# Two-layer decoder trunk on one core: eight wide expert places instead of twelve, ten expert groups instead of eleven, and the next layer's first weights prepared inside the expert stage

## The chip, the cores and the metric

The kernel runs on one core of a Trainium2 chip. The metric is the device time of one execution in microseconds (us). A trace of one execution shows for every engine what ran when: TensorE (PE, with its weight loads as PEld), VectorE (DVE), ScalarE (ACT), GpSimd (POOL), and SyncE (SP), whose queue issues nearly all transfers from device memory.

## The reference

Two layers over 256 tokens of width 1024, all in float32. Each layer mixes tokens (a combined projection, differential attention, sparse attention over 64 chosen keys, two gated branches, an output projection), normalises, and then runs a mixture of experts:

```
def hierarchical_moe(x, w_rg, b_rg, w_re, b_re, w_g, w_u, w_d):
    ...
    within = jnp.sum(jax.nn.one_hot(e_idx, EXPERTS_PER_GROUP, dtype=jnp.float32) * e_val[..., None], axis=1)
    comb = jax.nn.one_hot(g_idx[:, 0], N_GROUPS, dtype=jnp.float32)[:, :, None] * (g_val * within)[:, None, :]
    y = jnp.zeros_like(xt)
    for g in range(N_GROUPS):
        hg = jax.nn.silu(jnp.einsum('nd,edf->nef', xt, w_g[g])) * jnp.einsum('nd,edf->nef', xt, w_u[g])
        y = y + jnp.einsum('nef,efd->nd', hg * comb[:, g, :, None].astype(hg.dtype), w_d[g])
    return y.reshape(B, S, D)
...
        ple = jax.nn.sigmoid(x @ w_ple_gate[i]) * (p[i] @ w_ple[i])
        x = layer_norm(ALPHA * x + ffn + ple, ln2_g[i], ln2_b[i])
```

Every token goes to two of 32 experts (4 groups of 8; first one group, then two experts in it). On the reference's inputs the routing, worked out on the host from the reference alone, gives these tokens per expert. First layer: experts 0 to 3 have 45, 20, 35, 15; the four fullest of the others 45, 39, 28, 25; the next 23. Second layer: 13, 11, 12, 6; then 39, 39, 33, 32; the next 28.

## The kernel before

**Weights and places.** All weights lie in `ws` as blocks of 128 x 1024 float32, 512 KB each. The on-chip memory is cut into 47 places of that size (`Arena`, `Held`). A load takes the place that has been free longest (`load=True`); anything else takes one freed recently (`young=4` from the newest). SP issues the loads in one order, and each waits until the last reader of its place is done; what stands behind it in the queue waits too.

**The expert stage.** Experts are ranked: the first `NFIX` experts keep ranks 0 to 5 by number, so that their weights can be loaded before the routing is known, and the others follow by how many tokens they have. Ranks below `NBIG` have 64 columns, the others 32. A group fills 128 columns: two experts of 64 (12 loads) or four of 32 (24 loads). With 12 wide ranks that makes six groups of two and five of four, taken in the order `order`. Whatever does not fit in the columns is done by a loop over all experts, `leftover`, which is skipped when nothing is left over.

Each turn `gi` of the group loop runs on PE: `front(gi + 1)` (64 products of gate and up weights, which need 4 loads for each expert), `back(gi)` (32 products of the down weights, 2 loads for each expert), the gathering of the tokens for group `gi + 2`, and the combination of the group's result into the sums `ya` in PSUM. At some turns (`e1`, `early`, `lastat`) it also runs `Embed` units: a quarter of the per-layer embedding, two loads each and one more for two of them. `Embed(0)` is loaded early, and `nemb` says how many more are loaded before the routing is known.

**Before the routing is known** SP issues the loads of the fixed ranks and the early embeddings. Then it waits for `ids`, the ranks in a row, which `value_load` reads (L1034).

**End of a layer.** In the turn before the last, `wide` (L379) loads the two vectors of the second normalisation (queue line L382); POOL spreads them over the partitions. In the last turn the first four loads of the next layer's first projection are issued (`ahead`). Behind the last products the sums are normalised (`Norm`, L402 to L414), turned (L95), and the next layer's first projection begins. Each of its eight weight blocks is split into a rounded part and a rest (`parts`, `split`, L208 and L209): ACT makes the first, and here POOL the second.

Of the kernel before, what the change touches and what calls it, by code (L numbers as in the profile page):

```python
# [21 lines left out]
D = 1024  # L22
S = 256
DEPTH = 2
P = 128
KT = D // P
# [15 lines left out]
FAR = 1000.0  # L42


NFIX = 6
NBIG = 12


SEC = ["iq", "sq", "sk", "sv", "dq", "dk", "dv", "ga0", "ga1", "gb0", "gb1"]
# [30 lines left out]

@with_exitstack
def tile_hybrid_trunk(ctx: ExitStack, tc: tile.TileContext, x_in, xT_in, pT_in, pos_in, ws, wik, wrt, lnv,
                      brt, lamv, sublnv, out, places=47, t2b=4, young=4, gsb=1, hTb=1, silb=2, nring=5, early=(4, 5, 6), nahead=4, apart=8, npre=36, wA=1, wB=1, wC=1, wD=1, wE=3, inorder=2, e0=2, e1=2,  nearly_=0, peng_=1, ifat=3, im=0, df=0, dh=15, nol=0, diag=1, rpool='0000', lastemb=1, lastat=6, pre_if=(4,5), npair=6, fh=False, fg=0, order=(0,1,2,6,3,7,4,8,5,9,10), engs=None, nemb=1, nwarm=9, nfine=2, nah=4, o1=False, o2=False, o3=True, o4=True, order2=True, pa=2, pb=7, f1=True):
    nc = tc.nc
    V, A, G = nc.vector, nc.scalar, nc.gpsimd

    class Tensor:

        last = None
# [9 lines left out]
    def behind(*instructions):  # L99

        c = ExitStack()
        for i in instructions:
            if i is not None:
                c.enter_context(tc.issue_after(i.ins))
        return c

    def in_turn():

        return tc.issue_after(PE.last.ins)
# [14 lines left out]
    def bank():  # L124
        return ps.tile([P, 512], F32, tag="mm", bufs=4, name=nm("mm"))

    def wt(shape, dt, tag, bufs):
        return wk.tile(shape, dt, tag=tag, bufs=bufs, name=nm(tag))
# [3 lines left out]
    class Held:  # L132
# [11 lines left out]
        def free(self):  # L144
            arena.give(self.b)
# [16 lines left out]
    def load(l, i, shape):  # L162
        r = Held(shape, load=True)
        nc.sync.dma_start(r.t, ws[l, i])
        return r
# [41 lines left out]
    def split(hi, lo, src, eng=V):  # L207
        copied[0] = A.activation(hi, src, AF.Copy)  # L208
        copied[1] = eng.tensor_tensor(lo, src, hi, op=OP.subtract)  # L209
# [12 lines left out]
    ahead, ready = [], []  # L222
    nearly, peng = nearly_, peng_
# [30 lines left out]
    def constants():  # L254
# [14 lines left out]
        G.iota(kbon, pattern=[[-1, NE]], base=NE - 1, channel_multiplier=0, allow_small_or_imprecise_dtypes=True)  # L269
        V.tensor_scalar(kbon[:, :NFIX], kbon[:, :NFIX], 1.0e6, None, op0=OP.add)  # L270
        G.iota(kid[:, 0:1], pattern=[[0, 1]], base=0, channel_multiplier=1, allow_small_or_imprecise_dtypes=True)
        V.tensor_scalar(kid[:, 1:2], kid[:, 0:1], float(NFIX), 1.0e6, op0=OP.is_lt, op1=OP.mult)
        V.tensor_tensor(kid[:, 1:2], kid[:, 1:2], kid[:, 0:1], op=OP.subtract)
# [52 lines left out]
    def parts(w, ring=None, eng=V, old=False):  # L326

        if ring:
            ring.append(ring.pop(0))
        r = Held([2, 512], F32R, load=old, place=ring[-1] if ring else None)  # L330
        split(r.v[:, 0, :], r.v[:, 1, :], w, eng)
        return r
# [45 lines left out]

    def wide(i, l):  # L379

        r = Held([D])
        nc.sync.dma_start(r.v[0:1], lnv[l, i:i + 1])  # L382
        G.partition_broadcast(r.v, r.v[0:1])  # L383
        return r
# [68 lines left out]
    for l in range(DEPTH):  # L453
# [3 lines left out]
        ahead, ready = [], []  # L457
# [252 lines left out]
                free(*gates[:2])  # L710
        free(yaT, ybT)
        lng, lnb = wide(0, l), wide(1, l)
        wr36 = Held([KT, 36])
        nc.sync.dma_start(wr36.v, wrt[l])
        o = [None, None]
        for h in range(2):
# [161 lines left out]
        groups = [[(r, 2, 64)] for r in range(0, 2 * npair, 2)]  # L878
        small = NBIG
        for r in range(2 * npair, NBIG):  # L880
            n = min(2, NE - small)
# [69 lines left out]
        places = bank()  # L951
# [5 lines left out]
        with in_turn():  # L957
            places_of(places, mkf[:, :, :NFIX], slice(0, NFIX))
        gs = marks_of(0)
        with tc.issue_after(marked[0].ins):  # L960
# [24 lines left out]
            V.tensor_scalar(perm, iom[:NE, :NE], FAR, kcol[:, 2:3], op0=OP.add, op1=OP.is_equal)  # L985
            V.tensor_copy(cw[:, :, :NFIX], cbf[:, :, :NFIX])
        with in_turn():
# [8 lines left out]
        cmi = ids[:, NE:]  # L996
        V.tensor_scalar(ids[:, :NFIX], iom[0:1, :NFIX], FAR, None, op0=OP.add)
        V.tensor_copy(ids[:, NFIX:NE], b[0:1, 2 * NE + NFIX:3 * NE])
        over = cut(NE, rows=1)
        for c, n in (slice(0, NBIG), 64.0), (slice(NBIG, NE), 32.0):  # L1000
            V.tensor_scalar(over[:, c], b[0:1, 3 * NE + c.start:3 * NE + c.stop], n, None, op0=OP.subtract)
# [61 lines left out]
        def halves_of(yp):  # L1063
            y = t2([P, 512], F32R), t2([P, 512], F32R)
            split(*y, yp)
            return y
# [48 lines left out]
                        fetch(r, j)  # L1115
        for q in range(1, 1 + nemb):
            emb[q] = Embed(q)

        def strips(gi):


            for i, (_, sl) in enumerate(experts(gi)):
                for c in range(sl.start, sl.stop, 32):
                    yield i, slice(c, c + 32)
# [16 lines left out]
        def back(gi, hT):  # L1141

            ysplit.clear()
            ysplits.clear()
            wr = weights_of(gi, range(4, 6))
            if gi == last and l < DEPTH - 1:
                ahead.extend(load(l + 1, i, [2, 512]) for i in range(len(ahead), KT // 2))
                ready.extend(parts(r.v[:, k, :], eng=G) for r in ahead[:nearly] for k in range(2))
            ys = []
            for h in range(2):  # L1150
                yp = bank()
                for f in range(2):
                    for i, sl in strips(gi):
                        PE.matmul(yp[sl, :], hT[:, f, sl], wr[f][i].v[:, h, :], start=f == 0, stop=f == 1)
                ys.append(halves_of(yp))
                ysplits.append(copied[0])
                ysplit.append(copied[1])
            free(*wr[0], *wr[1])
            return ys

        last = len(groups) - 1
        ysplit, ysplits, powers = [], [], []
# [20 lines left out]
        def leftover(most):  # L1183
# [3 lines left out]
            with tc.If(most > 0, preferred_fallthrough_block=False):  # L1187
                onward(slice(0, NBIG), -64)
                onward(slice(NBIG, NE), -32)
                with tc.For_i(0, 2, 1):  # L1190
                    with tc.For_i(0, NE, 1) as r:
                        rest(r)
                    onward(slice(0, NE), -P)
                onward(slice(0, NBIG), 64 + 2 * P)
                onward(slice(NBIG, NE), 32 + 2 * P)
# [8 lines left out]
        for gi in range(len(groups)):  # L1204
            if gi == ifat:
                most = nc.values_load(cmi[0:1, 0:1], min_val=0, max_val=S)
            here = lambda: tc.manual_schedule(engines={mybir.EngineType.PE})
            with here():
                after = front(gi + 1, *slots) if gi < last else None
            if gi == ifat:  # L1210
                leftover(most)
            with here():
                ys = back(gi, hT)
                if gi + 2 <= last:
                    marks, slots = marks_of(gi + 2), Gathered(gi + 2 >= fg)
                    for k4 in range(2):
                        gather(marks, slots.half[k4], k4)
                units = embeds(gi)
                for e, t, some in units[:1]:
                    e.products(t, some)  # L1220
                if gi < last:
                    hT = turned(after[0], wt([P, 2 * P], F32, "hT", hTb))
                    for h in range(2):
                        for t in range(TT):
                            combine(ys[h], sT, h, t)
                    sT = after[1]
                for e, t, _ in units[:1]:
                    e.gate(t)
                for e, t, some in units[1:]:
                    e.products(t, some)  # L1230
                    e.gate(t)
                if gi + 2 <= last:
                    slots = slots, *ways_of(gi + 2, marks)
                for e, t, _ in units:
                    e.add(t)
            if gi == last - 1:
                lng, lnb = wide(2, l), wide(3, l)
                xn = [Held([D]) for _ in range(TT)]
                if l < DEPTH - 1:
                    xT = Split(KT)  # L1240
# [24 lines left out]
            ends[t:] = [norm.apply(t, o2)]  # L1265
            powers.append(power)
        lasts = copied[:]
        if l < DEPTH - 1:
            for k in range(KT):
                with behind(ysplits[min(k, 1)], powers[0] if k >= pa else None, powers[1] if k >= pb else None):  # L1270
                    ready.append(parts(ahead[k // 2].v[:, k % 2, :], eng=G, old=True))
            free(*ahead)

        free(lng, lnb, *x)
        x = xn

# [66 lines left out]
```

## Time and profile before

| | |
|---|---|
| three runs: median, lowest, highest | 939.35, 938.26, 940.98 us |
| the profiled execution | 940.85 us, of which 939.2 us span |
| PE busy | 906.3 us (96% of the span) |
| DVE, ACT, POOL busy | 425.7, 347.9, 33.8 us |
| bytes moved | 280.86 MB, 299 GB/s in the mean |

The expert stages lie from about 225 to 460 us and from about 687 to 926 us. PE counts as busy while a product runs or waits in its pipeline, so that 96% says little of what it waits for. The profile's row of GB/s shows where transfers run at their highest rate (about 416 GB/s) and where they do not.

### The profile page before, as it was taken

The page shows a single profiled execution, that of the slowest core. Times are in us where ns is not written, and L with a number is a line of the kernel's source. Part 1 is how long each engine was busy: PE and PEld are TensorE (multiplying, and loading weights), DVE is VectorE, ACT ScalarE, POOL GpSimd, SP SyncE. Part 2 cuts the span into 40 slices and gives each one's busy share as a digit, 9 for nine tenths or more (in the row PEclk, how much of TensorE's full clock was granted, in tenths as well). Part 3 has the DMA queues.
Part 4 walks back from the last instruction along what each step waited for, and adds up shares of the span by engine and source line. Part 5 has one row for each costly group of instructions (what it writes and reads, how often), then busy time and mean ns, then how long its engine had stood idle before and what let it go on. Part 6 is the DMA issues. An engine that isn't in the chain of part 4 may idle for free. (4 is left out here: it accounts for less than half of the span.)

```text
span 939.2 us, 15942 instructions
## 1 busy us (share of the span) xinstructions
PE 906.3 (96%) x5761; PEld 604.4 (64%) x5761; DVE 425.7 (45%) x1068; ACT 347.9 (37%) x704; POOL 33.8 (4%) x37
## 2 busy tenths in 40 slices
PE   8999999999999999999899999999989999999994
PEld 5877777876556466554388777788855465666441
DVE  6797466775221111122468954668731212112124
ACT  6567676532211111111346666775221111111110
POOL 0000000000000000000410000001000000000010
PEclk9999999999999999999999999999999999999998
DMA  8995343777899999996999233357778999999943
GB/s 280 414 405 202 115 144 127 248 235 286 304 380 385 412 418 416 416 415 273 387 418 364 90 125 123 113 186 252 251 278 322 360 417 414 418 419 416 418 177 139
DMA packets 79013, 280.86 MB, mean 299 GB/s; under 512 B 9160, under 2 KB 9928, under 8 KB 78928
## 3 DMA queue, kind: packets, MB, share of 16 engines
q1 hardware_dynamic: 78784, 279.78, 77.9%
q8 instruction: 47, 0.77, 0.3%
q14 instruction: 38, 0.31, 0.1%
q10 hardware_dynamic: 144, 0.00, 0.0%
HBM read 278.70 MB, written 1.05 MB: 298 GB/s over the span
## 5 line engine op out<-in xcount | busy, mean ns | idle before, releaser
L92 PE MATMUL acc<-a,a 128*128 128x512 f32 x1440 | 352.3, 398 | 2.7 <-ACT a L208 2.0
L92 PEld LDWEIGHTS acc<-a,a 128*128 128x128 f32 x1440 | 265.7, 188 | 65.5 <-ACT a L208 3.3
L92 PE MATMUL mm<-a,a 128*32 128x512 f32 (+5 forms) x1776 | 237.6, 526 | 0.0
L208 ACT ACTIVATE a<-a 128x512 fp32r<-128x512 f32 (+1 forms) x247 | 150.7, 631 | 100.2 <-PE acc L92 69.2
L209 DVE TENSOR_TENSOR a<-a,a 128x512 fp32r<-128x512 f32 (+1 forms) x239 | 160.1, 690 | 51.2 <-ACT a L208 50.5
L92 PEld LDWEIGHTS mm<-a,a 128*32 128x32 f32 (+3 forms) x1776 | 110.7, 130 | 99.2 <-issue 86.8
L92 PE MATMUL mm<-a,hT 128*32 128x512 f32 x704 | 96.4, 603 | 8.8 <-DMA a<-ws 4.9
L92 PEld LDWEIGHTS mm<-gs,a 128*128 128x128 f32 x704 | 80.4, 192 | 17.2 <-PE mm L92 11.7
L92 PE MATMUL mm<-gs,a 128*128 128x128 f32 x704 | 84.7, 278 | 0.0
L1050 ACT ACTIVATE sil<-mm 128x256 f32<-128x256 f32 x22 | 8.4, 383 | 171.5 <-PE mm L92 156.2
L92 PEld LDWEIGHTS mm<-a,hT 128*32 128x32 f32 x704 | 25.3, 111 | 71.4 <-issue 55.9
L1051 DVE SCALAR_TENSOR_TENSOR sil<-sil,wsl,mm 128x256 f32<-128x256 f32 x22 | 10.6, 481 | 133.6 <-ACT sil L1050 133.4
L209 DVE TENSOR_TENSOR t<-mm,t 128x512 fp32r<-128x512 f32 x44 | 30.4, 692 | 68.6 <-ACT t L208 68.6
L208 ACT ACTIVATE t<-mm 128x512 fp32r<-128x512 f32 x44 | 26.3, 597 | 78.6 <-PE mm L92 78.6
L919 DVE CAST sT<-mm 128x256 fp32r<-128x256 f32 x22 | 9.3, 425 | 97.4 <-PE mm L92 97.4
L92 PE MATMUL acc<-t,sT 128*128 128x512 f32 x176 | 48.4, 410 | 0.0
L906 ACT ACTIVATE a<-mm 128x512 f32<-128x512 f32 x40 | 23.9, 597 | 50.1 <-PE mm L92 47.6
L92 PEld LDWEIGHTS acc<-t,sT 128*128 128x128 f32 x176 | 31.1, 189 | 9.0 <-issue 2.5
L763 DVE TENSOR_TENSOR sil<-sil,mm 128x256 f32<-128x256 f32 x16 | 6.7, 416 | 54.4 <-ACT sil L762 54.4
L548 ACT ACTIVATE t<-mm,mx 128x128 f32<-128x128 f32 (+1 forms) x64 | 26.0, 421 | 10.7 <-DVE mx L545 10.7
L762 ACT ACTIVATE sil<-mm 128x256 f32<-128x256 f32 x16 | 6.1, 383 | 63.7 <-PE mm L92 63.7
L383 POOL PARTITION_BROADCAST a<-a x8 | 10.6, 1356 | 511.0 <-DMA a<-lnv 279.6
(197 smaller groups left out, 644.6 us busy)
## 6 DMA issues: line engine op xcount, KB each, us to landing
a<-ws SPq DMA_DIRECT2D x523, 512.0 KB, 9.4
a<-x_in SPq DMA_DIRECT2D x2, 512.0 KB
out<-a SPq DMA_DIRECT2D x4, 256.0 KB, 2.7
a<-xT_in SPq DMA_DIRECT2D x3, 256.0 KB
a<-wik SPq DMA_DIRECT2D x2, 288.0 KB, 8.2
a<-ws SPq DMA_DIRECT2D x2, 256.0 KB, 4.3
pT<-pT_in SPq DMA_DIRECT2D x2, 256.0 KB
a<-wrt SPq DMA_DIRECT2D x2, 144.0 KB, 2.7
```

Source lines behind the costliest of these rows:

```text
L92: self.last = nc.tensor.matmul(*a, **k)
L208: copied[0] = A.activation(hi, src, AF.Copy)
L209: copied[1] = eng.tensor_tensor(lo, src, hi, op=OP.subtract)
L383: G.partition_broadcast(r.v, r.v[0:1])
L548: A.activation(e[:, i * nk:(i + 1) * nk], b[:, i * nk:(i + 1) * nk], AF.Exp, bias=mx[:, i:i + 1], accum_out=sums[i])
L762: A.activation(g, b[:, :256], AF.Sigmoid)
L763: V.tensor_tensor(g, g, b[:, 256:], op=OP.mult)
L906: A.activation(xg, b.rearrange("p (k s) -> p k s", k=4), AF.Copy)
L919: V.tensor_copy(sT, b[:, :2 * P].rearrange("p (t q) -> p t q", t=TT))
L1050: A.activation(sil, gu[:, :FE], AF.Sigmoid)
L1051: V.scalar_tensor_tensor(sil, sil, wsl, gu[:, :FE], op0=OP.mult, op1=OP.mult)
```

## The change

Four ranks instead of six are fixed and eight instead of twelve have 64 columns. That makes four groups of two experts and six of four: ten groups. The three later embeddings are loaded before the routing is known and run one turn earlier, and so are the next layer's four first loads. The split of these is done in turns 6 and 7 by ACT and DVE, and no longer after the last group by ACT and POOL. The vectors of both normalisations and the routing weights (`wide`, `wr36`) take the longest free place, as loads do.

```
-NFIX = 6
-NBIG = 12
+NFIX = 4
+NBIG = 8
...
-  early=(4, 5, 6), lastat=6, pre_if=(4,5), npair=6, order=(0,1,2,6,3,7,4,8,5,9,10), nemb=1
+  early=(3, 4, 5), lastat=5, pre_if=(6,7), npair=4, order=(0,1,2,4,3,5,6,7,8,9), nemb=3
...
     def wide(i, l):
-        r = Held([D])
+        r = Held([D], load=True)
...
-        wr36 = Held([KT, 36])
+        wr36 = Held([KT, 36], load=True)
...
         for q in range(1, 1 + nemb):
             emb[q] = Embed(q)
+        if l < DEPTH - 1:
+            ahead.extend(load(l + 1, i, [2, 512]) for i in range(KT // 2))
...
             wr = weights_of(gi, range(4, 6))
-            if gi == last and l < DEPTH - 1:
-                ahead.extend(load(l + 1, i, [2, 512]) for i in range(len(ahead), KT // 2))
-                ready.extend(parts(r.v[:, k, :], eng=G) for r in ahead[:nearly] for k in range(2))
...
                 for e, t, _ in units:
                     e.add(t)
+            if l < DEPTH - 1 and gi in pre_if:
+                for r in ahead[:2] if gi == pre_if[0] else ahead[2:]:
+                    ready.extend(parts(r.v[:, k, :]) for k in range(2))
+                    r.free()
             if gi == last - 1:
...
         lasts = copied[:]
-        if l < DEPTH - 1:
-            for k in range(KT):
-                with behind(ysplits[min(k, 1)], powers[0] if k >= pa else None, powers[1] if k >= pb else None):
-                    ready.append(parts(ahead[k // 2].v[:, k % 2, :], eng=G, old=True))
-            free(*ahead)
```

(The changed parameters are shown without the ones that stay.)

How the order moves, at two places. First SP's queue in the first layer, just ahead of the wait for `ids`. Before, a<-ws of L1040 are expert weights and the last one of L164 is an embedding's:

```order
L1040 DMA a_2299<-ws 128x1024
L1040 DMA a_2301<-ws 128x1024
L1040 DMA a_2303<-ws 128x1024
L1040 DMA a_2305<-ws 128x1024
L164 DMA a_2311<-ws 128x1024
L1034 TENSOR_LOAD ids_2224
```

With the change the rows of L164 are embeddings and, the last four, the next layer's first weights:

```order
L164 DMA a_2291<-ws 128x1024
L164 DMA a_2293<-ws 128x1024
L164 DMA a_2295<-ws 128x1024
L164 DMA a_2297<-ws 128x1024
L164 DMA a_2299<-ws 128x1024
L164 DMA a_2301<-ws 128x1024
L164 DMA a_2303<-ws 128x1024
L164 DMA a_2305<-ws 128x1024
L1034 TENSOR_LOAD ids_2224
```

So 38 blocks are issued ahead of the wait (24 of experts, 10 of embeddings, 4 of the next layer) where 41 were (36 and 5); in the second layer 34 where 41 were.

Second, the split of the next layer's first weights. Before it is POOL's, between the two powers (L405) of the normalisation that ends the first layer (a_4401 to a_4407 are the four loads):

```order
L209 TENSOR_TENSOR a_4512<-a_4401,a_4512 128x512
L209 TENSOR_TENSOR a_4515<-a_4401,a_4515 128x512
L405 TENSOR_TENSOR rs_4438<-rs_4438,few 128x1
L209 TENSOR_TENSOR a_4518<-a_4403,a_4518 128x512
L209 TENSOR_TENSOR a_4521<-a_4403,a_4521 128x512
L209 TENSOR_TENSOR a_4524<-a_4405,a_4524 128x512
L209 TENSOR_TENSOR a_4527<-a_4405,a_4527 128x512
L209 TENSOR_TENSOR a_4530<-a_4407,a_4530 128x512
L405 TENSOR_TENSOR rs_4438<-rs_4438,few 128x1
L209 TENSOR_TENSOR a_4533<-a_4407,a_4533 128x512
```

With the change ACT's half stands in turns 6 and 7, here turn 6 (a_2299 and a_2301 are two of the loads; t_742 and t_745 belong to `back(6)`, L906 to the gathering):

```order
L208 ACTIVATE t_742_3848<-mm_3839 128x512
L208 ACTIVATE a_3923<-a_2301 128x512
L208 ACTIVATE a_3914<-a_2299 128x512
L208 ACTIVATE t_745_3861<-mm_3852 128x512
L208 ACTIVATE a_3917<-a_2299 128x512
L208 ACTIVATE a_3920<-a_2301 128x512
L906 ACTIVATE a_3867<-mm_3868 128x512
```

The eight operations of ACT stand between those of `back` and the gathering, four to a turn; their other halves are DVE's, and POOL has none.

## Rows read from the trace of the kernel before

**Rows 1.** Windows: stretch, busy us (count) of PE, PEld, DVE, ACT, POOL, clock, DMA share, GB/s

```profile
240.00:264.00 24.00, 23.51 (x208) 14.20 (x212) 4.77 (x13) 4.62 (x9) 0.00 (x0) 1.00 0.87 322
264.00:288.00 24.00, 24.00 (x216) 11.19 (x212) 4.56 (x12) 3.93 (x8) 0.00 (x0) 1.00 0.94 351
288.00:312.00 24.00, 23.64 (x162) 15.13 (x154) 3.63 (x9) 3.99 (x10) 0.00 (x0) 1.00 1.03 416
312.00:336.00 24.00, 22.27 (x177) 10.54 (x178) 5.67 (x14) 3.82 (x9) 0.00 (x0) 0.93 1.03 413
...
696.00:720.00 24.00, 22.26 (x201) 11.88 (x201) 6.05 (x18) 5.42 (x9) 0.00 (x0) 1.00 0.85 309
720.00:744.00 24.00, 24.00 (x205) 13.96 (x208) 4.73 (x14) 4.52 (x9) 0.00 (x0) 1.00 0.95 376
744.00:768.00 24.00, 24.00 (x172) 15.40 (x163) 4.53 (x11) 4.66 (x10) 0.00 (x0) 1.00 1.00 385
```

**Rows 2.** Waits of SP's queue in the second expert stage (us in total, times, longest)

```profile
SPq L382 <- PE mm L92: 16.0, 1, 16.0
```

**Rows 3.** Timeline of SP's queue, ends of both expert stages (start, us, how many)

```profile
425.03 5.73 SPq L1040 DMA_DIRECT2D a<-ws  x5
...
445.54 3.11 SPq L1040 DMA_DIRECT2D a<-ws  x6
448.69 2.38 SPq L164 DMA_DIRECT2D a<-ws  x4
...
885.27 7.85 SPq L1040 DMA_DIRECT2D a<-ws  x7
...
912.02 3.12 SPq L1040 DMA_DIRECT2D a<-ws  x6
```

**Rows 4.** Timeline of PE at the ends of both expert stages (in brackets, what PE waited for)

```profile
446.99 1.05 PE L92 MATMUL mm<-a,hT 128*32 128x512 f32 x2
...
456.68 2.76 PE L92 MATMUL mm<-a,hT 128*32 128x512 f32 x18 [0.22 <-DMA a<-ws]
...
913.47 1.05 PE L92 MATMUL mm<-a,hT 128*32 128x512 f32 x2
...
922.97 2.76 PE L92 MATMUL mm<-a,hT 128*32 128x512 f32 x18 [0.16 <-DMA a<-ws]
```

**Rows 5.** Timeline of PE, two starts of a turn of the group loop

```profile
244.96 7.07 PE L92 MATMUL mm<-a,a 128*32 128x512 f32 x64
...
261.80 7.07 PE L92 MATMUL mm<-a,a 128*32 128x512 f32 x64
```

**Rows 6.** The page, DMA issues: count, KB each, us from issue to landing

```profile
a<-ws SPq DMA_DIRECT2D x523, 512.0 KB, 9.4
```

**Rows 7.** Timeline of PE, gathering (mm<-gs,a) and an embedding unit

```profile
335.82 3.84 PE L92 MATMUL mm<-gs,a 128*128 128x128 f32 x32
...
345.90 3.61 PE L92 MATMUL mm<-a,a 128*128 128x256 f32 x16
```

**Rows 8.** The page, groups: the split of 128x512 blocks (busy us, mean ns)

```profile
L209 DVE TENSOR_TENSOR a<-a,a 128x512 fp32r<-128x512 f32 (+1 forms) x239 | 160.1, 690 | 51.2 <-ACT a L208 50.5
L208 ACT ACTIVATE a<-a 128x512 fp32r<-128x512 f32 (+1 forms) x247 | 150.7, 631 | 100.2 <-PE acc L92 69.2
```

**Rows 9.** Timelines behind the last groups: DVE in both layers, POOL and PE in the first

```profile
464.57 3.45 DVE L414 SCALAR_TENSOR_TENSOR a<-a,rs,a 128x512 f32<-128x512 f32 x2
933.90 1.41 DVE L414 SCALAR_TENSOR_TENSOR a<-a,rs,a 128x512 f32<-128x512 f32 x2
464.52 7.33 POOL L209 TENSOR_TENSOR a<-a,a 128x512 fp32r<-128x512 f32 x5
470.25 4.13 PE L92 MATMUL acc<-a,a 128*128 128x512 f32 x17
```

**Rows 10.** Timeline of PE behind the check for leftovers, both layers

```profile
313.73 5.31 PE L92 MATMUL mm<-a,hT 128*32 128x512 f32 x32 [2.09 <-DVEq L1187]
776.15 3.64 PE L92 MATMUL mm<-a,hT 128*32 128x512 f32 x32 [1.86 <-DVEq L1187]
```

More of the change, by code (lines that the diff above doesn't have):

```diff
@@ L82, in tile_hybrid_trunk @@
 def tile_hybrid_trunk(ctx: ExitStack, tc: tile.TileContext, x_in, xT_in, pT_in, pos_in, ws, wik, wrt, lnv,
-                      brt, lamv, sublnv, out, places=47, t2b=4, young=4, gsb=1, hTb=1, silb=2, nring=5, early=(4, 5, 6), nahead=4, apart=8, npre=36, wA=1, wB=1, wC=1, wD=1, wE=3, inorder=2, e0=2, e1=2,  nearly_=0, peng_=1, ifat=3, im=0, df=0, dh=15, nol=0, diag=1, rpool='0000', lastemb=1, lastat=6, pre_if=(4,5), npair=6, fh=False, fg=0, order=(0,1,2,6,3,7,4,8,5,9,10), engs=None, nemb=1, nwarm=9, nfine=2, nah=4, o1=False, o2=False, o3=True, o4=True, order2=True, pa=2, pb=7, f1=True):
+                      brt, lamv, sublnv, out, places=47, t2b=4, young=4, gsb=1, hTb=1, silb=2, nring=5, early=(3, 4, 5), nahead=4, apart=8, npre=36, wA=1, wB=1, wC=1, wD=1, wE=3, inorder=2, e0=2, e1=2,  nearly_=0, peng_=1, ifat=3, im=0, df=0, dh=15, nol=0, diag=1, rpool='0000', lastemb=1, lastat=5, pre_if=(6,7), npair=4, fh=False, fg=0, order=(0,1,2,4,3,5,6,7,8,9), engs=None, nemb=3, nwarm=9, nfine=2, nah=4, o1=False, o2=False, o3=True, o4=True, order2=True, pa=2, pb=7, f1=True):
     nc = tc.nc
```

## Prediction

> **What bounds the kernel now.** I began with the table: PE counts as busy for 96% of the span, which says only that it always has a product in its pipeline. So I read the two expert stages by windows next, because there the change moves transfers and turns. In the first stage the transfer rate is 322 and 351 GB/s from 240 to 288 us and then 416 and 413; in the second it is 309, 376 and 385 from 696 to 768 us [rows 1]. At full rate a block of 512 KB (524,288 bytes at 416 GB/s) takes 1.26 us. The reader should see that the full rate is a ceiling and that the low windows leave room below it.
>
> The third view is the wait list of SP's queue: at L382, the two vectors of the second normalisation, it stands still once in the second stage for 16.0 us behind PE [rows 2]. The queue's timeline shows what that does. In the first stage five expert loads are issued from 425.03 on, up to 430.76 (425.03 + 5.73); the next six follow only at 445.54, and four loads of the next layer at 448.69. In the second stage issuing ends at 893.12 (885.27 + 7.85) and the last six expert loads come at 912.02 [rows 3]. PE's timeline shows the price. The last group's back products start at 446.99 and 913.47, but their last 18 run only from 456.68 to 459.44 and from 922.97 to 925.73, each time behind a load [rows 4]; the same 32 products take 3.64 us where nothing stops them [rows 10]. So the stages are bound by PE nearly to the end, and the end by loads that a waiting queue has let go too late.
>
> **The change part by part.** *One group less.* Two starts of a turn lie 16.84 us apart (261.80 - 244.96) [rows 5]. Without one turn PE could begin its last back at 430.2 and 896.6. But the loads don't become fewer. First layer: before, 41 go out ahead of the routing, then 161, then the four of the next layer: 206. After: 38 + 168 = 206. Second layer: 41 + 161 = 202, and 34 + 168 = 202. So the loads decide how much of 16.84 us is kept.
>
> *Late places for the two vectors.* They take the place that has been free longest, whose last reader lies in the front of the last group but one, some 1.5 turns back. The queue then does not stop, and the loads behind it follow at the full rate. I count from the last issue before the stop, half a microsecond before the end of its row (six issues take 3.11 us): 430.2 and 892.6. From issue to landing is 9.4 us [rows 6].
> First layer: 430.2 + 9.4 = 439.6; ten loads are left (six and four), 10 x 1.26 = 12.6, so the last lands at 452.2.
> Second layer: 892.6 + 9.4 = 902.0; six are left, 7.5, so 909.5.
> Both lie after the time at which PE could be there (430.2, 896.6): the stage is then bound by loads, and most of the group that is saved turns into waiting for them.
>
> *Fewer loads ahead of the routing* (three and seven). They must be caught up at the start of the stage. The room there is (416-322 + 416-351) GB/s x 24 us = 3.8 MB, 7.3 loads, in the first layer; (107 + 40 + 31) x 24 = 4.3 MB, 8.2 loads, in the second [rows 1]. Three and seven fit. Cost 0; if nothing is caught up, 3 x 1.26 + 7 x 1.26 = 12.6 us.
>
> *Embeddings one turn earlier, beside groups of four.* While PE gathers and runs an embedding, no place of an expert comes free: from 335.82 to the middle of the unit at 345.90 it is 11.9 us [rows 7], of which 9.4 are covered by loads in flight [rows 6]. Two such pauses in a layer would give 5 us of idle transfers, none gives 0; I take 2 us a layer.
>
> With that and the last 18 products (2.76 us) [rows 4] the last back ends at 452.2 + 2 + 2.76 = 457.0, where it was 459.44: -2.4. In the second layer 909.5 + 2 + 2.76 = 914.3 where it was 925.73: -11.4. The first layer gains little because the four loads of the next layer, which came behind the last expert weights, now come ahead of them.
>
> *The split of the next layer's weights.* It leaves POOL. In the first layer POOL's splits begin at 464.52, and beside them DVE takes 3.45 us for two operations of L414 that take 1.41 in the second layer, where POOL has nothing to do [rows 9]: -2.0. In turns 6 and 7 there are now four operations of ACT (0.63) and four of DVE (0.69) each [rows 8]. These engines are busy for about 4 to 5 of 24 us there [rows 1], and what waits for them is covered by the gathering (3.84) [rows 7]. I take 0; without the cover it is 4 x 0.63 = 2.5 us a turn, 5 in all.
>
> *The rest costs nothing.* The vectors' spreading on POOL stays early by more than a turn; the same rule for `wr36` and the first normalisation's vectors touches queue entries outside the stages, behind which the loads have long been issued. If they gain or lose, it is bounded by one issue-to-landing time, 9.4 us, and I give that no part of the sum.
>
> **Sum.** -2.4 - 11.4 - 2.0 = -15.8 us. The profiled execution took 940.85; 925.0 then. That execution lies 1.5 above the median of the three runs (939.35), so the forecast is 923.5.
>
> **The rivals.** *The stream does not catch up.* Then the ten loads cost 12.6 us and the time is 936.1. For it: four next-layer blocks and more embeddings now sit in places from before the routing on, so fewer places turn over when the stage starts. Against it: the room of 7.3 and 8.2 loads above, and that two groups of four in the middle leave PE waiting while transfers run full.
>
> *The clock falls while PE waits.* After 2.09 us of waiting at 313.73, 32 back products took 5.31 us, in a window with a granted clock of 0.93; after 1.86 us at 776.15 they took 3.64 [rows 1, 10]. So a short wait can bring a stretch at the lower of the clock's two levels (1.2 instead of 2.4 GHz), and the new waits come in many small pieces. What runs while loads are missing is hidden; what follows is not: if the last 2.76 us double in each layer [rows 4], and the first 4.13 us of the next layer too [rows 9], it is +9.7: 933.2. Against it: in the rows of the ends PE waits for loads already, and its 18 products take the same 2.76 twice.
> The Trainium skill, page "TensorE: Matmul & The Clock Gate", section "HAM oscillation — how this bites in real kernels", describes just this: a kernel whose products are shorter than its wait for the next weights runs every burst at half clock. By that rule this rival holds and the time is 933.2; the two ends shown do not bear it out, the check for leftovers in the first layer does.
>
> *Slower: too few places for groups of four.* A group of four needs 24 loads, the next-layer blocks hold four places from the routing to turns 6 and 7, and their split parts then hold eight of the 47 to the end. If the queue therefore waits for places as at 240 us, a window of 24 us runs at 322 GB/s instead of 416 [rows 1], 4.3 loads or 5.4 us. Three such windows eat the gain (16.2); four make it slower. In each of the last four groups of both layers it is 8 x 5.4 = 43: 966.7. Against it: the windows from 288 on, where groups of four alternate with pairs, run full.
>
> *PE is the bound after all,* because loads run ahead more than I count. Then the last back ends at 446.99 - 16.84 + 3.64 = 433.8 (-25.6) and at 900.3 (-25.5); with 2.0 the time is 886.3. The rate of 416, which no window exceeds, speaks against it.
>
> *Something is left over.* If an expert has more tokens than its columns, `leftover` runs over all experts, hundreds of us. The counts of the reference exclude it: with eight wide ranks no expert below them has over 32 (23 and 28 at most), and the fixed and wide ones at most 45 of 64.
>
> **How the numbers follow.** Chances: forecast 0.65; not caught up 0.12; clock 0.08; too few places 0.11; PE bound 0.03; left over 0.01. The forecast's own range is 914 to 931: without pauses 4 lower, and 5 lower again if the early queue entries give half of their 9.4 us; with pauses of 5 instead of 2 it is 6 higher, and a little more with half of the uncovered splits. For 8 in 10 I reach down to 913 and up to 937, which takes in the first two rivals. About 0.3% (2.8 us) is what a measurement can tell from no change. Faster: 0.65, 0.08 of the clock, 0.03 of PE and a third of "not caught up" (936.1 lies just under the line of 936.5, so most of its spread counts as the same): 0.80. Same: 0.08. Slower: 0.12.
>
> **What the changed profile would show.** Right: no wait of SP at L382; the last back products end near 457 minus what shifts ahead of it, and near 914 minus the first layer's gain; PE's waits for loads grow by 10 to 20 us a layer; windows at 416 GB/s from about 285 and 750 us up to the stages' ends; L414 at about 0.7 us each in both layers; no split on POOL. Wrong: windows below 400 late in the stages (too few places), back products of 5 us with a clock below 1.00 at the ends (clock), SP still waiting at L382 (the change does not do what it says), or last backs that end near 434 and 900 (PE).

## The result, and the profile after

| | before | changed |
|---|---|---|
| median of four runs | 940.16 us | 929.54 us |
| lowest, highest | 938.26, 942.28 us | 927.54, 930.63 us |
| the profiled execution (span) | 940.85 (939.2) us | 927.54 (925.7) us |

The ratio is 0.9884 (95% interval 0.9855 to 0.9913): about 11 us or 1.2% faster. On another chip it was 0.989 (0.9872 to 0.9907). The profiled execution of the changed kernel is the fastest of its four, so the two profiles lie 13.3 us apart and the medians 10.6.

SP's queue in the changed kernel, at the ends of both stages (answers to [rows 3]):

```profile
415.36 19.24 SPq L1040 DMA_DIRECT2D a<-ws  x16
435.45 1.51 SPq L382 DMA_DIRECT2D a<-lnv  x2
438.31 7.38 SPq L1040 DMA_DIRECT2D a<-ws  x8
...
875.03 14.10 SPq L1040 DMA_DIRECT2D a<-ws  x12
889.99 1.52 SPq L382 DMA_DIRECT2D a<-lnv  x2
892.58 7.86 SPq L1040 DMA_DIRECT2D a<-ws  x8
```

Each stretch begins within 1.4 us of the end of the one ahead of it: the queue no longer stands still at L382 here. (Outside the stages it waits more there than before: behind DVE 17.7 us in the whole execution where it was 4.3, at the first normalisation's vectors. The large loads of L164 wait less behind DVE, 92.9 us where it was 112.1.) PE at the same places ([rows 4]; the third row is the first long stretch of the next layer, which stood at 470.25 in [rows 9]):

```profile
452.98 1.05 PE L92 MATMUL mm<-a,hT 128*32 128x512 f32 x2 [0.22 <-DMA a<-ws]
454.25 2.76 PE L92 MATMUL mm<-a,hT 128*32 128x512 f32 x18 [0.23 <-DMA a<-ws]
...
465.46 4.09 PE L92 MATMUL acc<-a,a 128*128 128x512 f32 x17
...
908.19 1.04 PE L92 MATMUL mm<-a,hT 128*32 128x512 f32 x2 [0.20 <-DMA a<-ws]
909.41 2.76 PE L92 MATMUL mm<-a,hT 128*32 128x512 f32 x18 [0.17 <-DMA a<-ws]
```

The first layer's last back ends at 457.01 (454.25 + 2.76), the second's at 912.17. Just ahead of these last 18, products come in pairs, each pair 1.2 to 1.3 us behind the last: PE now runs at the pace at which blocks land. Windows ([rows 1]; the columns are the same):

```profile
240.00:264.00 24.00, 23.18 (x204) 14.17 (x208) 5.07 (x14) 4.63 (x9) 0.00 (x0) 1.00 0.96 374
264.00:288.00 24.00, 24.00 (x216) 11.10 (x210) 4.56 (x12) 3.60 (x8) 0.00 (x0) 1.00 0.96 350
...
312.00:336.00 24.00, 21.94 (x142) 15.86 (x146) 5.60 (x15) 4.65 (x10) 0.00 (x0) 1.00 1.02 399
336.00:360.00 24.00, 24.00 (x171) 16.12 (x164) 3.13 (x6) 4.23 (x9) 0.00 (x0) 1.00 1.00 392
...
432.00:456.00 24.00, 21.39 (x87) 4.74 (x86) 2.33 (x5) 2.45 (x5) 2.48 (x2) 1.00 1.03 417
...
768.00:792.00 24.00, 21.42 (x136) 14.65 (x129) 3.56 (x7) 3.85 (x8) 0.00 (x0) 1.00 0.98 393
792.00:816.00 24.00, 24.00 (x175) 14.36 (x174) 5.17 (x14) 4.65 (x10) 0.00 (x0) 1.00 0.98 376
```

The last stretch of the first stage runs at 417 GB/s; the dips at 312 to 360 and 768 to 816 lie where the embeddings now run. The split of the next layer's weights has left the tail, and the two operations of L414 take 1.41 us in the first layer too (the timeline of DVE):

```profile
461.44 1.41 DVE L414 SCALAR_TENSOR_TENSOR a<-a,rs,a 128x512 f32<-128x512 f32 x2
```

One thing is new that the prediction had put at nothing. The spreading of the *first* normalisation's vectors, at 183 and 188 us in the kernel before, now runs on POOL at 93 and 97 us, amid the softmax of the sparse attention. POOL's and DVE's timelines of the changed kernel there:

```profile
97.06 1.30 POOL L383 PARTITION_BROADCAST a<-a  x1 [2.67 <-DVE sums L578]
```

```profile
97.09 1.68 DVE L581 TENSOR_SCALAR t<-t,sums 128x256 f32<-128x256 f32 x2
```

and DVE's in the kernel before, where POOL has nothing to do then:

```profile
97.47 0.62 DVE L581 TENSOR_SCALAR t<-t,sums 128x256 f32<-128x256 f32 x2
```

PE waits for L581 for 4.3 us in the whole execution (total, times, longest), where it was 1.2:

```profile
PE mm L95 <- DVE t L581: 4.3, 4, 1.4
```

### The profile page after: what moved, and what is told of

Same layout as the page of the kernel before. It is cut to its first block, busy times and chain, and to the rows that moved or that the text cites. A ratio compares the mean times of both kernels' runs of the same rounds, so it can differ in the third digit from the quotient of the medians.

```text
span 925.7 us, 15402 instructions
## 1 busy us (share of the span) xinstructions
PE 890.5 (96%) x5473; PEld 588.0 (64%) x5473; DVE 423.5 (46%) x1064; ACT 341.6 (37%) x692; POOL 22.2 (2%) x29
## 3 DMA queue, kind: packets, MB, share of 16 engines
HBM read 278.70 MB, written 1.05 MB: 302 GB/s over the span
## 5 line engine op out<-in xcount | busy, mean ns | idle before, releaser
L92 PE MATMUL mm<-a,a 128*32 128x512 f32 (+5 forms) x1648 | 229.2, 521 | 1.2 <-DMA a<-ws 1.1
L209 DVE TENSOR_TENSOR a<-a,a 128x512 fp32r<-128x512 f32 (+1 forms) x247 | 164.8, 688 | 50.8 <-ACT a L208 49.9
L92 PEld LDWEIGHTS mm<-a,a 128*32 128x32 f32 (+3 forms) x1648 | 107.4, 132 | 96.9 <-issue 78.0
L92 PE MATMUL mm<-a,hT 128*32 128x512 f32 x640 | 102.9, 594 | 10.1 <-DMA a<-ws 5.3
L92 PEld LDWEIGHTS mm<-gs,a 128*128 128x128 f32 x640 | 73.1, 192 | 15.5 <-PE mm L92 10.9
L92 PE MATMUL mm<-gs,a 128*128 128x128 f32 x640 | 77.0, 278 | 0.0
L209 DVE TENSOR_TENSOR t<-mm,t 128x512 fp32r<-128x512 f32 x40 | 27.6, 691 | 76.6 <-ACT t L208 76.6
L92 PE MATMUL acc<-t,sT 128*128 128x512 f32 x160 | 43.8, 410 | 0.0
L906 ACT ACTIVATE a<-mm 128x512 f32<-128x512 f32 x36 | 21.5, 597 | 43.1 <-PE mm L92 41.7
L92 PEld LDWEIGHTS acc<-t,sT 128*128 128x128 f32 x160 | 28.3, 189 | 7.4 <-issue 1.7
L95 PE MATMUL mm<-identr,t 128*128 128x128 f32 (+1 forms) x132 | 21.8, 278 | 4.3 <-DVE t L581 4.3
```

The costliest lines, as they stand in the source:

```text
L92: self.last = nc.tensor.matmul(*a, **k)
L95: self.last = nc.tensor.transpose(*a, **k)
L906: A.activation(xg, b.rearrange("p (k s) -> p k s", k=4), AF.Copy)
```

## The experiments

Two theories. By the **queue theory** (the prediction's own) the time comes from the queue that no longer stops at L382, and the group that is saved goes into waiting for loads. By the **group theory** it comes from the turn that PE no longer runs. Later a third was added for the loss: by the **port theory** POOL's work beside the softmax holds DVE up.

**Late places alone.** One edit to the kernel before:

```
     def wide(i, l):
-        r = Held([D])
+        r = Held([D], load=True)
```

> The kernel before, in which only the late places for the two vectors are taken over (eleven groups, splits on POOL behind the last group). Queue theory: what the change brings comes from the queue that no longer stands still at L382, and the saved group goes into waiting for loads. Then this one edit is enough: expert loads end by 430.2 + 9.4 + 7.5 = 447.1, so the last back runs at PE's own time, 446.99 to 450.6 (-8.8), in the second layer 913.5 to 917.1 (-8.6): about 17 us less than before, 921 to 926 us, no slower than the whole change (929.5). Group theory: the gain is the turn that PE no longer runs; then this edit alone brings less than half of it, 935 to 940 us.

Measured: 928.52 us, ratio 0.984 (0.9801 to 0.9879). This one edit gives at least what the change gives (0.9884). PE's waits from 228 to 460 us name no load at all; the last backs begin without a wait:

```profile
449.51 4.39 PE L92 MATMUL mm<-a,hT 128*32 128x512 f32 x32
...
909.63 3.64 PE L92 MATMUL mm<-a,hT 128*32 128x512 f32 x32
```

The group theory falls: with eleven groups PE has one turn more to run, and the time is as short. The time is 2.5 us above the upper end of what was expected, but the kernel before read 942.84 in this comparison; the ratio stands for about 15 us of the 17.

**The queue made to stop again.** The changed kernel with recently freed places for the vectors and for `wr36`:

```
-        r = Held([D], load=True)
+        r = Held([D])
...
-        wr36 = Held([KT, 36], load=True)
+        wr36 = Held([KT, 36])
```

> The changed kernel with recently freed places for the vectors and the routing weights again. Queue theory: the queue stands still once more, now behind the back of the last group but one, and the last six to ten loads come late; by the row of before (eleven us from the first issue behind the stop to the start of the last 18 products) the last back ends near 460 and 916 instead of 457.0 and 912.2: 7 us slower than the changed kernel, 935 to 938 us. Group theory: no difference beyond 1.5 us, 928 to 931 us.

Measured: 935.99 us, 0.9928 (0.9898 to 0.9958), as the queue theory has it. By the ratios it is 4 us slower than the changed kernel (0.9884), not 7, because the edit also takes the first vectors out of the softmax. The run with late places for the second vectors only, below, differs from this one in these places alone and has 0.9851: the stop costs about 7 us. The last backs end at 463.72 and 921.53, later than expected. SP's wait list and, below it, PE's last 18 products of both stages:

```profile
SPq L382 <- PE mm L92: 13.9, 2, 7.0
```

```profile
460.96 2.76 PE L92 MATMUL mm<-a,hT 128*32 128x512 f32 x18 [0.20 <-DMA a<-ws]
...
918.77 2.76 PE L92 MATMUL mm<-a,hT 128*32 128x512 f32 x18 [0.18 <-DMA a<-ws]
```

The two stops are 13.9 us together, at most 7.0; in the second stage it was 16.0 [rows 2]. PE now waits for loads itself when the queue gets there, so the back that the queue waits for is not as far behind the loads; this reason is read from the rows and not tested.

**The next layer's blocks last.** The changed kernel, with the four loads and their split at their old places:

```
-        if l < DEPTH - 1:
-            ahead.extend(load(l + 1, i, [2, 512]) for i in range(KT // 2))
...
             wr = weights_of(gi, range(4, 6))
+            if gi == last and l < DEPTH - 1:
+                ahead.extend(load(l + 1, i, [2, 512]) for i in range(len(ahead), KT // 2))
...
-            if l < DEPTH - 1 and gi in pre_if:
-                for r in ahead[:2] if gi == pre_if[0] else ahead[2:]:
-                    ready.extend(parts(r.v[:, k, :]) for k in range(2))
-                    r.free()
```

and the loop with `eng=G` behind the last group is put back.

> The changed kernel with the next layer's first four blocks loaded in the last turn and split by ACT and POOL behind the last group, as before; ten groups, early embeddings and late places stay. If loads bound the first stage, the four blocks no longer stand ahead of the last expert weights: the last back of the first layer ends 4 x 1.26 = 5.0 us earlier, near 452, and POOL's split beside DVE costs 2.0 to 2.4 again: 2.6 us faster than the changed kernel, 925 to 928 us. If the early split is what counts and the loads do not, it is 2 us slower, 931 to 933 us.

Measured: 926.65 us, 0.9831 (0.9792 to 0.9871), faster as expected, though its interval and the change's overlap a little. The last back ends at 451.50, and L414 has its price again:

```profile
448.74 2.76 PE L92 MATMUL mm<-a,hT 128*32 128x512 f32 x18 [0.19 <-DMA a<-ws]
```

```profile
456.47 2.88 DVE L414 SCALAR_TENSOR_TENSOR a<-a,rs,a 128x512 f32<-128x512 f32 x2
```

So the early blocks cost the first stage 4.8 us (228.6 against 223.8 in the table below, both at full clock) and win back 1.7 in the tail: from the last back to the next layer's first long stretch it is 10.1 us here and 8.45 in the changed kernel.

**The split off POOL, but not early.** The run with late places alone, with the split behind the last group given to DVE:

```
-                    ready.append(parts(ahead[k // 2].v[:, k % 2, :], eng=G, old=True))
+                    ready.append(parts(ahead[k // 2].v[:, k % 2, :], old=True))
```

> The kernel before with the late places for the two vectors, and POOL's half of the split behind the last group given to DVE. If POOL beside DVE is what makes two operations of L414 take 3.45 instead of 1.41 us, they take 1.41 here and the kernel is 1 to 2.4 us faster than the one with the late places alone. If the eight splits of 0.69 us on DVE push the normalisation back instead, it is up to 5.5 us slower than that one.

Measured: 927.93 us, 0.9841 (0.9803 to 0.9879): no different from the run without it. Half of the expectation holds, L414 takes 1.41 us again; the other half shows why that wins nothing here:

```profile
457.58 0.64 DVE L209 TENSOR_TENSOR a<-a,a 128x512 fp32r<-128x512 f32 x1
458.13 0.15 DVE L404 TENSOR_SCALAR rs<-mv 128x1 f32<-128x1 f32 x1
458.19 1.40 DVE L413 SCALAR_TENSOR_TENSOR a<-acc,mv,a 128x512 f32<-128x512 f32 x2
459.51 1.41 DVE L414 SCALAR_TENSOR_TENSOR a<-a,rs,a 128x512 f32<-128x512 f32 x2
```

DVE's splits stand between the steps of the normalisation. Counted from the end of the last back, L413 begins 0.76 us later than in the run without this edit (458.19 - 453.78 against 457.55 - 453.90), and the next layer's first long stretch 0.5 us later (10.57 against 10.05 us), although L414 is 1.4 us shorter. The change shortens the tail because the split is gone from there, not because it left POOL.

**The changed kernel again**, beside the next three on one chip.

> The changed kernel as it is, timed beside the variants of this group on one chip. Both theories: its ratio to the kernel before is again near 0.988, about 11 us less, within the scatter of some 1.5 us.

Measured: 930.2 us, 0.989 (0.9872 to 0.9907). Its profile shows a second execution of the changed kernel, of 930.05 us; the last back of the first layer and the next layer's first long stretch stand there at

```profile
456.54 2.76 PE L92 MATMUL mm<-a,hT 128*32 128x512 f32 x18 [0.21 <-DMA a<-ws]
467.75 4.11 PE L92 MATMUL acc<-a,a 128*128 128x512 f32 x17
```

so the last back ends at 459.30, and not at 457.01.

**Late places for the second normalisation's vectors only.**

```
-        r = Held([D], load=True)
+        r = Held([D], load=i > 1)
...
-        wr36 = Held([KT, 36], load=True)
+        wr36 = Held([KT, 36])
```

> The changed kernel with late places for the second normalisation's two vectors alone; the first normalisation's vectors and the routing weights take recently freed places again. Port theory: the late places let POOL spread the first vectors amid the softmax, where two operations of L581 took 1.68 us instead of 0.62; here POOL is back behind the softmax, PE waits 1.2 us for L581 instead of 4.3, and the kernel is about 3 us faster than the changed one, 925 to 928 us. Queue theory against it: the early queue entries no longer let expert loads by, fewer of them are ahead when the stage starts, and the time stays or is up to 5 us longer.

Measured: 927.04 us, 0.9851 (0.9832 to 0.987), 3.2 us below the changed kernel beside it. PE's wait list:

```profile
PE mm L95 <- DVE t L581: 1.2, 2, 0.6
```

The port theory holds: it is the placing of the first vectors, which the change moved along, that cost 3 us. This edit also takes back the late place of `wr36`, so by itself it does not part the two. The run with late places alone has no late `wr36`, and PE waits 4.5 us for L581 there; in the run with eleven groups and late second vectors only, below, it is 1.1 us. The wait goes with the vectors.

**Both edits together:** the blocks last, and late places for the second vectors only.

> The two edits together that should help: the next layer's blocks loaded last, as in the run with the blocks last, and late places for the second normalisation's vectors alone. If both theories hold, it is faster than either: about 3 us below the run with the blocks last, 6 us below the changed kernel, 922 to 925 us. If the early entries of the queue matter for the prefetch, it is no faster than the run with the blocks last.

Measured: 923.96 us, 0.9825 (0.9808 to 0.9843), as expected: the two edits add up.

**A group of four earlier.** The changed kernel with

```
-order=(0,1,2,4,3,5,6,7,8,9)
+order=(0,1,4,2,5,3,6,7,8,9)
```

> The changed kernel with the first group of four moved ahead by one group (order 0,1,4,2,5,3 in place of 0,1,2,4,3,5). If loads bound the stages, what counts is that transfers run full from the stage's start: the windows of 374 and 350 GB/s at 240 to 288 us rise to 416, up to 4.9 loads or 6 us less in the first layer and little in the second, 923 to 928 us. If PE's turns bound the stages, or the transfers lose as much later, it is the same, 928 to 931 us.

Measured: 926.54 us, 0.9847 (0.983 to 0.9864), 3.7 us below the changed kernel. Its windows from 240 to 288 us run at 384 and 386 GB/s, not at 416, and those at 312 and 336 at 416 and 417: part of the gain comes from the embeddings' pauses, which a fuller stream covers. That was not in the expectation.

**The kernel before with late places for the second vectors only,** a single edit and eleven groups:

```
-        r = Held([D])
+        r = Held([D], load=i > 1)
```

> The kernel before with one edit: late places for the second normalisation's two vectors alone; eleven groups and all else stay. Queue and port theory together: the run with all late places, of which PE never waited for expert weights, less the 3 us that PE then waits for L581: 921 to 924 us by a kernel before of 940, faster than the whole change (930). Group theory: the change with the same late places (927) stays ahead.

Measured: 924.31 us, 0.9824 (0.98 to 0.9847). It is a hair above what was expected and well ahead of the whole change. It is also level with the run of both edits together (ten groups, blocks last, second vectors late: 0.9825): once the queue does not stop, the saved group and what came along with it bring nothing that can be measured until the order is changed as well.

**All that helped, together:** blocks last, second vectors only, the group of four earlier.

> The version with the blocks last and late places for the second vectors alone, and the first group of four moved ahead by one group. Its transfers run at 380 to 405 GB/s in four windows of 24 us; if loads bound the ten groups and the earlier four-group fills those windows, it is 2 to 4 us faster, 920 to 922 us. If they are embeddings' pauses that stay, it is the same, 923 to 925 us.

Measured: 920.85 us, 0.9777 (0.9752 to 0.9802), the fastest version of the study. Its windows:

```profile
240.00:264.00 24.00, 22.58 (x206) 12.88 (x195) 4.66 (x12) 5.01 (x10) 0.00 (x0) 1.00 1.02 415
264.00:288.00 24.00, 24.00 (x211) 12.04 (x213) 4.72 (x14) 3.05 (x6) 0.00 (x0) 1.00 1.03 416
...
336.00:360.00 24.00, 24.00 (x175) 14.36 (x174) 4.86 (x12) 4.65 (x10) 0.00 (x0) 1.00 1.03 418
...
792.00:816.00 24.00, 24.00 (x170) 15.63 (x170) 3.13 (x6) 3.85 (x8) 0.00 (x0) 1.00 1.03 416
```

All its windows of 24 us from 240 to 480 and from 696 to 888 us lie between 410 and 419 GB/s: transfers run full through the stages. That the bytes are then all that is left to save there follows from this and was not tested.

**Two places fewer.** The changed kernel with `places=45`:

> The changed kernel with 45 places for blocks instead of 47. If loads bound the stages at the full rate, two loads fewer are on the chip when each stage starts: 2 x 1.26 us in each layer, 5 us slower, 934 to 937 us. If too few places already slow the stream within the stages, it costs more than that, 940 us and over. If there is room to catch up, it is the same, 929 to 931 us.

Measured: 933.58 us, 0.9915 (0.9892 to 0.9939): 0.25% more than the changed kernel, less than expected. Part of that is an accident of the order: with 45 places PE waits only 1.2 us for L581, since POOL's spreading falls at 104.55 and 113.28 us there, and 3 us come back. The stages alone, in the table below, are 2.5 and 3.4 us longer than the changed kernel's, near the 2 x 1.26 us each of loads that fill the time.

The stages side by side, from the start of the first group's products (mm<-a,t) to the end of the last back, worked out from PE's timelines (us). The last column is what the 32 products behind the first layer's check for leftovers took: 3.6 at full clock, 5.3 at the lower one. These 1.7 us come and go between executions of one kernel (last section), and first stages are to be compared where they agree.

| version | groups | first stage | second stage | behind the first check |
|---|---|---|---|---|
| before | 11 | 231.4 | 235.0 | 5.3 |
| changed | 10 | 228.6 | 225.3 | 3.6 |
| changed, second execution | 10 | 230.7 | 225.3 | 5.3 |
| late places alone | 11 | 222.6 | 227.3 | 3.6 |
| queue stops again | 10 | 234.2 | 228.9 | 5.3 |
| second vectors late only | 10 | 231.3 | 225.1 | 5.3 |
| blocks last | 10 | 223.8 | 225.0 | 3.6 |
| 45 places | 10 | 231.1 | 228.7 | 3.6 |
| combined | 10 | 221.8 | 222.1 | 5.3 |

## Why the prediction was right

The forecast was 923.5 with a range of 913 to 937; 929.54 lies inside, the direction and the mechanism hold, and the sum was 5.2 us too large against the medians (15.8 forecast, 10.6 measured), 2.5 against the two profiles (13.3). The smaller miss is in part luck: the profile of before, from whose rows the sum was counted, has the lower clock behind the first check, and the first profile of the changed kernel has not. The second execution (930.05 us) has it too, and lies 10.8 us below before, as the medians do. With these two the terms come out like this (us):

| term | forecast | measured |
|---|---|---|
| end of the first layer's last back | -2.4 | -0.1 (459.44 to 459.30) |
| from there to the next layer's first long stretch | -2.0 | -2.4 (10.81 to 8.45) |
| from there to the start of the second stage | 0 | +1.2 (220.45 to 221.65) |
| the second stage | -11.4 | -9.7 (235.03 to 225.29) |
| sum | -15.8 | -11.0 |

*Loads bound the stages.* Right in kind; the first layer's term was about 2.3 us too large. Its last back was put at 457.0 and ended at 457.01 in the first profile, but that is luck: in the second execution it ended at 459.30.

*The saved turn becomes waiting.* Right, and shown by the table: with late places, ten groups instead of eleven gain 2.3 us in the second stage (227.3 to 225.0) and lose 1.2 in the first (both at full clock), where a turn is worth 16.84. PE's waits for loads add up to only 6.4 us in the list of the whole execution, where 10 to 20 a layer were announced. That was the wrong place to look: most of the waiting is counted as busy products that take 1.05 us a pair instead of 0.23 (3.64 us for sixteen pairs, [rows 10]).

*The catching up.* Right in the second layer: the window from 696 us runs at 417 GB/s, where it was 309 [rows 1]. In the first the windows from 240 to 288 run at 374 and 350, where they were 322 and 351: 1.2 MB, 2.3 of the three loads, were caught up there.

*The pauses of the embeddings.* A term that was mis-sized. I took 2 us a layer. By the windows of the first profile it is (17 + 24) GB/s x 24 us = 1.0 MB, 1.9 loads or 2.4 us, in the first layer, and (23 + 40) x 24 = 1.5 MB, 2.9 loads or 3.6 us, in the second; its stage gained 9.7 us where 11.4 were put down. In the second execution the same windows run at 381 and 390, and at 414 and 349 GB/s: 3.5 and 4.0 us. There, some 1.5 to 2 us a layer of the miss are this term.

*The split.* -2.0 was put down. From the last back's end to the first long stretch of the next layer it is 8.45 us (465.46 - 457.01), before 10.81 (470.25 - 459.44): -2.4. The reason given, POOL beside DVE, is only part of it, as the run with DVE's split shows.

*"The rest costs nothing."* The step that failed: a cost put at nothing, with one issue-to-landing time as its bound. I followed the queue entries of the first vectors and `wr36`, and not what hangs on them: POOL spreads the vectors as soon as they land, and landed 90 us earlier they meet the softmax. It costs about 1.5 us a layer; the second stage therefore starts only 3.8 us earlier than before (686.92 against 690.70), where the first layer's end had gained 4.8.

DVE's two operations begin at 97.09, while POOL runs from 97.06 to 98.36, and lose 1.06 us, nearly the broadcast's whole 1.30. It is the same in the other two overlaps of the changed kernel: each time DVE's pair of operations ends 0.39 to 0.41 us behind the broadcast (94.79 and 94.39, 98.77 and 98.36, 556.89 and 556.50), where both together take 0.62 alone. The Trainium skill, page "SBUF — State Buffer", section "SBUF: two separate sides", says that DVE and GpSimd share one pair of ports as an exclusive lock: whichever starts first keeps it for its whole instruction and the other is blocked. For DVE it names operations in a two-port mode and, against a GpSimd operation that reads SBUF, those with two inputs there. The rows agree with such a lock; which of these kinds L581 is, no row shows.

*The rivals.* The stream caught up, PE was not the bound, nothing was left over. (The rate that "no window exceeds" is 419 GB/s in the windows of before, not 416; nothing hangs on it.) The clock did not fall in the short waits: the last 18 products take 2.76 us in both layers, as before, and the granted clock is 1.00 from 432 to 456, where PE waits for blocks some 0.2 us at a time. The slower case, too few places, was real in kind and small in size: two places are worth 2.5 to 3.4 us a stage, so the blocks that sit there early cost something, but nothing like 5.4 us in each of eight windows.

Of the 2.7 us between the difference of the medians and that of the first two profiles, 1.7 are accounted for by the clock behind the first check. The rest, about 1 us, stays open; it is no larger than the scatter of single executions.

## What to carry to other kernels

When a queue issues everything in order, look first at which entry it stands still on: in each layer one small load with a badly chosen buffer held back the last six to ten large ones; the two stops together cost about 15 us, and one argument mended both. Where a stage is bound by bytes, taking work off the compute engine buys waiting, so compare stage lengths and not busy shares, and make sure that the clock was the same in both. And when a load moves earlier, follow what it sets off: a second engine that starts sooner may land on a busy stretch of a third.

## What the runs showed of the hardware

The same wait is not always followed by the same clock. Behind the check for leftovers in the first layer PE waits for 2.09 us; in the first profile of the changed kernel the 32 products behind it took 3.64 us, and in the second execution they took 5.34, in a window with a granted clock of 0.93:

```profile
314.29 5.34 PE L92 MATMUL mm<-a,hT 128*32 128x512 f32 x32 [2.09 <-DVEq L1186]
```

In the thirteen profiles of this study the wait there is 2.08 to 2.13 us; six then show 5.28 to 5.34 us and seven 3.64. Behind the same check in the second layer, after 1.86 to 1.95 us, none shows it. What decides between the two is not shown. So 1.7 us of a difference between two profiles can be this alone. The start of the program scatters as well: the first run of 55 products begins at 10.24 us in the changed kernel's profile and at 12.29 in that of the combined version, and takes 13.07 us in the first and 15.54 in the second, in code that is the same. In the profiles of this study the first stage begins anywhere from 227.1 to 231.8 us, so they are best compared by stage and not by their ends.
